# The lora outer products and the decay sum of an RWKV-7 layer, made per 512 tokens and passed through DRAM

## The chip, the cores and the metric

One core of one Trainium2 chip runs the whole program in one launch. The metric is device time in microseconds. The kernel before takes 3426.49 us (median of 3 runs, 3426.42 to 3430.7).

## The reference, cut to what matters

A two-layer decoder trunk over 1024 tokens of width 1024 in float32. Layer 0 mixes tokens with RWKV-7, layer 1 with gated DeltaNet; each is followed by a SwiGLU feed-forward of width 2816, with adaLN modulation and LayerNorm around them. The change touches layer 0 only:

```python
r = lerp(0) @ w_rkv[0]; k = lerp(1) @ w_rkv[1]; v = lerp(2) @ w_rkv[2]
w_log = -softplus(-(w0 + tanh(lerp(3) @ w1) @ w2)) - 0.5    # inner width 64
a = sigmoid(a0 + (lerp(4) @ a1) @ a2)                       # inner width 64
g = sigmoid(lerp(5) @ g1) @ g2                              # inner width 128
decay = exp(-exp(w_log))
# recurrence over tokens, per head of 64: S <- S*decay + (S a)b + v k
return (y * g) @ w_out
```

The three loras are `(… @ w1) @ w2`, `(… @ a1) @ a2` and `(… @ g1) @ g2`. Their first product is called the inner one, the second the outer one. The recurrence is run in chunks of 64 tokens; for that the kernel needs the running sum of `-log(decay)` inside each chunk, which it gets as a scan of `0.5*exp(-0.5)*(1 + tanh(z/2))`, with z the outer product plus `w0`.

## The kernel before, in words

Activations lie with channels on the 128 partitions (8 tiles `p` of 128 channels, each two heads) and tokens along the free dimension, in two halves `h` of 512 tokens. Every large product is done in three float32r matmuls (`mm3`, lines 261 to 263: high by high, high by low, low by high); weights are loaded by a DMA on SP's queue, cut into a high part by ACT (line 222 or 249) and a low part by POOL or DVE (line 212).

`proj_rwkv` makes, for each half, k, v and r in the order (h,1), (h,2), (h,0): for each `p` 24 matmuls of 512 columns into one PSUM bank `mm`, an ACT copy (line 471) and a store to DRAM (`rkv_d`, line 472). Beside v and r it accumulates the inner lora products in a bank `rows`, three matmuls of 512 columns for each `p`. At the end of a group the inner result `f` is cut into two parts kept in SBUF (`split_lora`).

The recurrence works on units: 256 tokens `q` of one `p` and half, 32 units in all, four of them in flight (`pairs`, with cut points `CUT`). `prep1` loads r, k, v from DRAM (line 994) and the norms (line 997), and builds the chunk matrices; `prep2` inverts; `chain` carries the state, normalizes, multiplies by the gate and stores `y` (line 1184). In the kernel before `prep1` also does, per unit, two `mm3` of 256 columns with the outer weights (loaded and cut at q == 0, line 1000), tanh on ACT, an affine step (line 196) and the scan (line 1024) on DVE; `chain` does a third `mm3` of 256 columns with the gate's weights (line 1171) into half of a PSUM bank `p1`.

The order of the instructions is written as Python generators that yield cost estimates; `weave` mixes two such generators by their estimated totals, and a list scheduler then orders each engine's queue ahead of time. On the chip every engine runs its queue in that fixed order. Four stretches matter here. First the projections of half 0 run alone, with the adaLN product (0 to about 235 us). Then the first 19 steps of the units are woven with the projections of half 1 (about 235 to 690). Then the other 16 steps are woven with layer 0's output projection and feed-forward of half 0 (to about 1380). Then the rest of layer 0 and layer 1.

Of the kernel before, what the change touches and what calls it, by code (L numbers as in the profile page):

```python
# [57 lines left out]
def body(ctx, tc, A):  # L58
# [23 lines left out]
    def tl(pl, shape, dt, tag, bufs=1):  # L82
        return pl.tile(shape, dt, tag=tag, name=nm(tag), bufs=bufs)
# [33 lines left out]
    def p1_ps():  # L117
        return bank("p1")
# [71 lines left out]
    def sigmoid(out, src, c=0.5, scale=0.5, hbias=None, d=None):  # L190

        if hbias is None:
            act.activation(out=out, in_=src, func=AF.Tanh, scale=scale)
        else:
            act.activation(out=out, in_=src, func=AF.Tanh, scale=scale, bias=hbias)
        dve.tensor_scalar(out=out, in0=out, scalar1=c, scalar2=c if d is None else d, op0=MUL, op1=ADD)
# [124 lines left out]
        return mod1[l][:, 24 * s + 16 + k:24 * s + 17 + k]  # L321

    rkv_d = [[[tl(dram, [P, HT], F32, f"rkv{h}{i}{p}") for p in range(KT)] for i in range(3)] for h in range(2)]
    y_d = [[[tl(dram, [P, HT], F32, f"y{l}{h}{p}") for p in range(KT)] for h in range(2)] for l in range(2)]
    kn_d = [tl(dram, [16, HT], F32, f"kn{h}") for h in range(2)]
    qk_d = [[tl(dram, [16, HT], F32, f"qk{h}{i}") for i in range(2)] for h in range(2)]
# [2 lines left out]
    A["taps"] = {"rkv": rkv_d, "y": y_d, "x2": x_d}  # L329

    utail = tl(cp, [P, KT], F32, "utail")

    lora = {}

    def sums(acc, sel, p, sq):

# [15 lines left out]
    def proj_rwkv():  # L352
# [88 lines left out]
        loaded.append(other_constants())  # L441
        for k in range(4, KT):
            lerp(0, 1, k)
        for (h, i), (h2, i2) in zip(order, order[1:]):
            a = [made[h, i, k] for k in range(KT)]
            acc = row_ps()
            for grp in GROUPS[h]:
                ws = {}
                for n in SMALL[i]:
                    lerp(h, 3 + n, grp[0])  # L450
                early = grp[0] in begun
                w = [None if early else weight(A["w_rkv"][i, p], (dve if p % SD[1] == 0 else pool) if h else None, ("r", i, p) if i != 1 or p >= NH else None) for p in grp]
                if h == 0:
                    ws = {n: small_weight(h, n, grp[0]) for n in SMALL[i]}
                pst = [begun.get(p) or mm_ps() for p in grp]
                if early:
                    half_product(grp[0], 1, ws0[grp[0]])
                    del begun[grp[0]]
                for k in range(KT):
                    for j in range(0 if early else len(grp)):  # L460
                        mm3(pst[j][:, :], w[j], P * k, a[k], k == 0, k == KT - 1)
                    if h and grp[-1] == KT - 1:
                        lerp(h2, i2, k)
                    if PY and k < KT - 1:
                        yield 0.65 * len(grp)
                for j, p in enumerate(grp):
                    if j:
                        for n in SMALL[i]:
                            lerp(h, 3 + n, p)
                    o = e_tile()  # L470
                    act.copy(out=o[:, :], in_=pst[j][:, :])
                    sync.dma_start(out=rkv_d[h][i][p][:, :], in_=o[:, :])
                    if i == 1:
                        sq = e_tile()
                        act.activation(out=sq[:, :], in_=pst[j][:, :], func=AF.Square, scale=V("kk", p))
                        sums(acc, C("hsel"), p, sq)
                    for n in SMALL[i]:
                        mm3(acc[:, :], ws.get(n) or small_weight(h, n, p), 0, made[h, 3 + n, p], p == 0 and n != 1, p == KT - 1 and n != 0)
                    if i == 0:
                        make_x(h + 1, p)  # L480
                    if h == 0:
                        lerp(h2, i2, p)
                    yield Part({1: 6.0, 2: 6.5, 0: 5.8}[i] - 7 * 0.65 * bool(PY))
            for k in range(KT):
                lerp(h2, i2, k)
            if i == 1:
                rows_out(kn_d[h], acc, 1e-6)
            else:
                f = inner[h, i] = tl(pools["pj"], [P, HT], F32, "f")
                if i == 2:  # L490
                    act.activation(out=f[0:64, :], in_=acc[0:64, :], func=AF.Tanh)
                    act.copy(out=f[64:P, :], in_=acc[64:P, :])
                else:
                    sigmoid(f[:, :], acc[:, :])
                if h == 0:
                    split_lora(h, i)

    loaded = []
    inner = {}

    def split_lora(h, i):

        t = lora.setdefault(h, {})
        f = inner.pop((h, i))
        t[i] = [tl(pools["l"], [P, HT], F32R, f"l{i}{e}")[:, :] for e in "hl"]
        split(f[:, :], *t[i])

    def lo_eng():
        flip[0] = (flip[0] + 1) % 3
# [215 lines left out]
          7: [1, 1, 1]}  # L725
    KNS = 17
    CS = [1.0, 1.0, 1.0]
    CUT = [14.0, 26.0, 41.0, 55.0]
    K = len(CUT)
    CUT[-1] = CUT[-1] + 0.0  # L730
    S2 = 3
# [2 lines left out]
    NC = [4, 3, 3, 3, 4]  # L734
    OP = ['u', '']
    NA = 0
    UC = 49.0
    GB = 1
    TI = 12
    TC = [1.0, 1.1, 1.0]  # L740
# [240 lines left out]
                live.remove(g)  # L981

    post_ps = {'p1': p1_ps, 'pa': pa_ps, 'pc': pc_ps, 'mm': mm_ps}['p1']
    gates = {}

    def prep1(rp, nb, ctxr, h, p, q, n, box):
        def r_tile(tag="t", n=nb["t"]):
            return tl(rp, [P, QT], F32, tag, n)

        tq = slice(QT * q, QT * q + QT)  # L990
        lrh, lrl = lora[h][2]
        r, k, v = r_tile("ld", nb["ld"]), r_tile("ld", nb["ld"]), r_tile("ld", nb["ld"])
        for i, t in ((1, k), (0, r), (2, v)):
            sync.dma_start(out=t[:, :], in_=rkv_d[h][i][p][:, tq])
        rb = r_tile("rb", 1)
        for j in range(2):
            sync.dma_start(out=rb[64 * j:64 * j + 64, :], in_=kn_d[h][2 * p + j:2 * p + j + 1, tq].to_broadcast([64, QT]))
        if q == 0:
            lw = tl(rp, [P, 2 * P], F32, "l2r", 1)
            sync.dma_start(out=lw[:, :], in_=A["w_l2"][p, :, 0:2 * P])  # L1000
            gates[p] = [(tl(rp, [P, 2 * P], F32R, "l2h", 2), tl(rp, [P, 2 * P], F32R, "l2l", 2))]
            split(lw[:, :], *(t[:, :] for t in gates[p][0]))
        wl2 = gates[p][0]
        lr = (lrh[:, tq], lrl[:, tq])
        pz = p1_ps()
        mm3(pz[:, 0:QT], wl2, 0, lr, True, True)
        dec = r_tile()
        if 'P' in OP[h]:
            act.activation(out=dec[:, :], in_=pz[:, 0:QT], func=AF.Tanh, scale=0.5, bias=vneg[:, p:p + 1])
            c = 0.5 * math.exp(-0.5)  # L1010
            pool.tensor_scalar(out=dec[:, :], in0=dec[:, :], scalar1=c, scalar2=c, op0=MUL, op1=ADD)
        elif 'd' in OP[h]:
            act.activation(out=dec[:, :], in_=pz[:, 0:QT], func=AF.Tanh, scale=0.5, bias=vneg[:, p:p + 1])
            act.activation(out=dec[:, :], in_=dec[:, :], func=AF.Identity, scale=0.5 * math.exp(-0.5), bias=bcol(5))
        else:
            sigmoid(dec[:, :], pz[:, 0:QT], c=0.5 * math.exp(-0.5), hbias=vneg[:, p:p + 1])
        yield 4.0
        pz = p1_ps()
        mm3(pz[:, 0:QT], wl2, P, lr, True, True)
        a = r_tile()  # L1020
        act.activation(out=a[:, :], in_=pz[:, 0:QT], func=AF.Tanh, scale=0.5, bias=vneg[:, 8 + p:9 + p])
        yield 1.0
        cum = r_tile()
        dve.tensor_tensor_scan(out=cum[:, :], data0=C("reset"), data1=dec[:, :], initial=0.0, op0=MUL, op1=ADD)
        e1 = tl(rp, [P, 4, 65], F32, "e1", nb["e1"])
        dve.memset(e1[:, :, 0:1], 1.0)
        act.activation(out=e1[:, :, 1:65], in_=v3(cum[:, :], 4), func=AF.Exp, scale=-1.0)
# [81 lines left out]
    def chain(rp, nb, ctxr, h, p, q, box):  # L1109
# [7 lines left out]
        for c in range(4):  # L1117
# [34 lines left out]
                stt(n0[hs, hs], pst[hs, hs], dcol[hs, c:c + 1], np_[hs, hs], MUL, ADD)  # L1152
            act.copy(out=yn[rr, P * i:P * i + P], in_=pq[rr, 0:P])
            yield 2.1
        y4 = v3(yn[:, :], 4)
        mean, var, tmp = (tl(rp, [P, 4], F32, n_, 2) for n_ in ("gm", "gv", "gt"))
        dve.tensor_reduce(out=mean[:, :], in_=y4, axis=mybir.AxisListType.X, op=ADD)
# [8 lines left out]
        newton(mean[:, :], var[:, :], tmp[:, :])  # L1166
        tt(dve, y4, y4, mean[:, :].unsqueeze(2).to_broadcast([P, 4, 64]), MUL)
        yield 2.1
        if q == 0:
            lw = tl(rp, [P, P], F32, "g2r", 1)  # L1170
            sync.dma_start(out=lw[:, :], in_=A["w_l2"][p, :, 2 * P:3 * P])
            gates[p].append((tl(rp, [P, P], F32R, "g2h", 2), tl(rp, [P, P], F32R, "g2l", 2)))
            split(lw[:, :], *(t[:, :] for t in gates[p][1]))
        wg = gates[p][1]
        lgh, lgl = lora[h][0]
        t = post_ps()
        for i in range(2):
            pe.transpose(t[:, P * i:P * i + P], yn[:, P * i:P * i + P], C("ident"))
        y = tl(rp, [P, QT], F32, "yo", nb["yo"])
        act.activation(out=y[:, :], in_=t[:, 0:QT], func=AF.Identity, bias=V("gnb", p), scale=V("gng", p))  # L1180
        tt(pool, y[:, :], y[:, :], bv[:, :], ADD)
        mm3(t[:, QT:2 * QT], wg, 0, (lgh[:, tq], lgl[:, tq]), True, True)
        tt(dve, y[:, :], y[:, :], t[:, QT:2 * QT], MUL)
        sync.dma_start(out=y_d[0][h][p][:, tq], in_=y[:, :])
        yield 4.2

    def pairs(rp, nb, ctxr):

# [260 lines left out]
    def main():  # L1449
        with tc.tile_pool(name="pj", bufs=1) as pools["pj"]:  # L1450
# [17 lines left out]
            steps = pairs(rp, nb, cr)  # L1468
            B = [2, 1, 1, 2, 2]
            banks(mm=B[0], rows=B[1], pa=B[2], p1=B[3], pc=B[4])  # L1470
            weave(seq(*steps[:SB]), 16 * UC * W[0], parts(proj, 3 * KT - PP), 112, LD[0])
            split_lora(1, 2)
            weave(seq(*steps[SB:SB + S2]), S2 * UC, proj, 34)
            split_lora(1, 0)
        pools["acc"] = ctx.enter_context(tc.tile_pool(name="acc", bufs=1, reuse_waits="tile"))
        B = [2, 1, 1, 2, 2]
        banks(mm=B[0], rows=B[1], pa=B[2], p1=B[3], pc=B[4])
# [138 lines left out]
```

## Time and profile before

| | |
|---|---|
| median of 3 runs | 3426.49 us |
| the profiled execution's own time | 3418.32 us |
| its span | 3416.5 us |
| TensorE busy | 3229.8 us, 19408 matmuls |
| DVE / ACT / POOL busy | 2207.9 / 1374.5 / 974.0 us |
| mean granted TensorE clock | 0.97 |
| moved by DMA | 594.12 MB |

PE is the matmul engine, PEld its weight loads, SPq the queue from which the DMAs are issued. A matmul's shown duration includes its pipeline, so neighbours overlap: what one takes from PE is read from the start of one matmul to the start of the next. "[5.58 <-ACT l2h L222]" behind a row says that the engine stood idle for 5.58 us before it and what it waited for.

### The profile page before, as it was taken

Reading aid. Unit: us, or ns where it says so; the run is one execution under the profiler, and the core shown is the slowest. Engines: PE = TensorE matmul, PEld = TensorE weight load, DVE = VectorE, ACT = ScalarE, POOL = GpSimd, SP = SyncE. Lnnn points to the kernel's source line nnn. Section 1 sums busy time; section 2 is a strip of 40 time slices with the busy share of each in tenths; the row PEclk is TensorE's granted clock in tenths of the full one; section 3 lists DMA queues with packets and bytes.
Section 4 is the critical chain, followed back from the end, with each engine's and each line's share of the span. In section 5 each row is a group of like instructions: output and inputs, shape, how many; then the busy total and the mean of one; then the engine's idle time right before and its main releaser. Section 6 shows DMA issues by size and latency. Waiting matters only on the chain. (4 is left out here: it accounts for less than half of the span.)

```text
span 3416.5 us, 51830 instructions
## 1 busy us (share of the span) xinstructions
PE 3229.8 (95%) x19408; PEld 2464.8 (72%) x19408; DVE 2207.9 (65%) x4630; ACT 1374.5 (40%) x2622; POOL 974.0 (29%) x725
## 2 busy tenths in 40 slices
PE   7989999988999999988999999999989999999997
PEld 3667777765666676766777777777767778878886
DVE  5667888877666666587676555586577763573235
ACT  4656777634333333344332222345323223342222
POOL 2443233343333333443321000220133333420001
PEclk8999999997999999999999999999999999999998
DMA  7872334352444444644664554556644446565543
GB/s 260 274 242 89 114 106 132 122 171 82 159 148 165 145 165 141 217 165 175 223 209 166 182 170 168 199 187 218 223 166 157 151 151 235 182 209 185 197 174 135
DMA packets 240524, 594.12 MB, mean 174 GB/s; under 512 B 24720, under 2 KB 80656, under 8 KB 240272
## 3 DMA queue, kind: packets, MB, share of 16 engines
q1 hardware_dynamic: 240128, 590.74, 51.1%
q8 instruction: 152, 2.49, 0.3%
q14 instruction: 100, 0.82, 0.1%
q10 hardware_dynamic: 144, 0.07, 0.0%
HBM read 440.04 MB, written 150.67 MB: 173 GB/s over the span
## 5 line engine op out<-in xcount | busy, mean ns | idle before, releaser
L261 PE MATMUL mm<-s,wh 128*128 128x512 f32 x2608 | 1081.3, 415 | 14.0 <-DVE s L224 5.9
L262 PE MATMUL mm<-s,wh 128*128 128x512 f32 x2608 | 1057.9, 406 | 14.6 <-DVE s L212 8.2
L263 PE MATMUL mm<-s,wl 128*128 128x512 f32 x2608 | 1050.0, 403 | 0.0
L212 POOL TENSOR_TENSOR wl<-wr,wh 128x1024 fp32r<-128x1024 f32 (+1 forms) x243 | 504.4, 2082 | 981.9 <-ACT wh L222 912.4
L261 PEld LDWEIGHTS mm<-s,wh 128*128 128x128 f32 x2608 | 497.4, 191 | 129.2 <-issue 19.8
L262 PEld LDWEIGHTS mm<-s,wh 128*128 128x128 f32 x2608 | 498.4, 191 | 112.3 <-DVE s L212 12.7
L263 PEld LDWEIGHTS mm<-s,wl 128*128 128x128 f32 x2608 | 497.5, 191 | 95.1 <-issue 1.2
L249 ACT CAST wh<-wr 128x1024 fp32r<-128x1024 f32 x199 | 206.6, 1049 | 500.4 <-PE mm L262 260.3
L222 ACT CAST wh<-wr 128x1024 fp32r<-128x1024 f32 (+1 forms) x254 | 228.2, 905 | 343.9 <-PE mm L262 201.1
L215 DVE SCALAR_TENSOR_TENSOR x<-mm,modp,x 128x512 f32<-128x512 f32 x272 | 202.1, 747 | 73.9 <-PE mm L263 72.0
L261 PE MATMUL mm<-ys,wh 128*128 128x512 f32 x544 | 219.6, 404 | 2.9 <-DVE x L215 2.8
L262 PE MATMUL mm<-ys,wh 128*128 128x512 f32 x544 | 217.3, 400 | 0.0
L263 PE MATMUL mm<-ys,wl 128*128 128x512 f32 x544 | 217.3, 399 | 0.0
L212 DVE TENSOR_TENSOR e<-mm,e 128x512 f32<-128x512 f32 x88 | 60.6, 689 | 168.7 <-PE mm L263 168.4
L212 DVE TENSOR_TENSOR s<-e,s 128x512 fp32r<-128x512 f32 x106 | 122.2, 1154 | 60.8 <-ACT s L222 60.6
L833 PEld LDWEIGHTS <-z 128*128 128x128 f16 x1600 | 83.8, 98 | 103.3 <-issue 64.2
L215 DVE SCALAR_TENSOR_TENSOR e<-e,mm 128x512 f32<-128x512 f32 x88 | 60.2, 684 | 141.8 <-ACT e L676 141.4
L215 DVE SCALAR_TENSOR_TENSOR tx<-mm,modp,tx 128x512 f32<-128x512 f32 x112 | 83.1, 748 | 79.4 <-PE mm L263 79.1
L261 PEld LDWEIGHTS mm<-ys,wh 128*128 128x128 f32 x544 | 103.7, 191 | 29.7 <-DVE x L215 3.7
L263 PEld LDWEIGHTS mm<-ys,wl 128*128 128x128 f32 x544 | 103.5, 190 | 25.7
L262 PEld LDWEIGHTS mm<-ys,wh 128*128 128x128 f32 x544 | 103.7, 191 | 25.2 <-issue 0.5
L215 DVE SCALAR_TENSOR_TENSOR e<-e,vec,e 128x512 f32<-128x512 f32 x144 | 115.0, 799 | 3.8
(389 smaller groups left out, 5418.8 us busy)
## 6 DMA issues: line engine op xcount, KB each, us to landing
wr<-w_in SPq DMA_DIRECT2D x176, 512.0 KB, 4.5
ada<-ada_w SPq DMA_DIRECT2D x96, 512.0 KB, 4.8
loi<-wl SPq DMA_DIRECT2D x88, 512.0 KB, 3.0
wr<-w_ffo SPq DMA_DIRECT2D x88, 512.0 KB, 4.9
wl<-loi SPq DMA_DIRECT2D x88, 512.0 KB, 3.6
wr<-w_g SPq DMA_DIRECT2D x64, 512.0 KB, 4.5
lof<-wl SPq DMA_DIRECT2D x44, 512.0 KB, 2.9
wl<-lof SPq DMA_DIRECT2D x44, 512.0 KB, 3.5
```

The lines of the kernel that those rows point to most:

```text
L212: eng.tensor_tensor(out=out, in0=a, in1=b, op=op)
L215: return dve.scalar_tensor_tensor(out=out, in0=a, scalar=s, in1=b, op0=op0, op1=op1)
L222: act.copy(out=hi, in_=src)
L249: act.copy(out=hi[:, :], in_=raw[:, :])
L261: pe.matmul(out, wh[:, off:off + P], ah, start=start, stop=False)
L262: pe.matmul(out, wh[:, off:off + P], al, start=False, stop=False)
L263: pe.matmul(out, wl[:, off:off + P], ah, start=False, stop=stop)
L833: pe.matmul(out, l, r, start=start, stop=stop)
```

## The change

A new DRAM array `lo_d` holds, for each half and `p`, the running sum, the tanh of `a` and the gate. `outer(h, i, p)` makes them for 512 tokens at a time, inside `proj_rwkv`; `prep1` and `chain` load 256 tokens of them for a unit. The inner parts are now in one pair of tiles, used by one lora after the other.

```diff
+        def outer(h, i, p):
+            n = 2 if i == 2 else 1
+            raw = tl(pools["pj"], [P, 2 * P], F32, "l2r")
+            sync.dma_start(out=raw[:, 0:P * n], in_=A["w_l2"][p, :, (0 if n == 2 else 2 * P):P * (2 if n == 2 else 3)])
+            w = [tl(pools["pj"], [P, 2 * P], F32R, "l2" + e) for e in "hl"]
+            split(raw[:, 0:P * n], *(t[:, 0:P * n] for t in w))
+            for j in range(n):
+                ps = mm_ps()
+                mm3(ps[:, :], w, P * j, inner[h, i], True, True)
+                o = e_tile()
+                if n == 1:
+                    act.copy(out=o, in_=ps[:, :])
+                elif j == 0:
+                    dec = e_tile()
+                    sigmoid(dec, ps[:, :], c=0.5 * math.exp(-0.5), hbias=vneg[:, p:p + 1])
+                    for q in range(2):
+                        tq = slice(256 * q, 256 * q + 256)
+                        dve.tensor_tensor_scan(out=o[:, tq], data0=C("reset"), data1=dec[:, tq], initial=0.0, op0=MUL, op1=ADD)
+                else:
+                    act.activation(out=o, in_=ps[:, :], func=AF.Tanh, scale=0.5, bias=vneg[:, 8 + p:9 + p])
+                sync.dma_start(out=lo_d[h][j if n == 2 else 2][p][:, :], in_=o)
+            yield 0.7 * n
...
                     yield Part({1: 6.0, 2: 6.5, 0: 5.8}[i] - 7 * 0.65 * bool(PY))
+                    if i == 0 and (h == 0 or p < 4):
+                        for pair in (p,) if h == 0 else (2 * p, 2 * p + 1):
+                            yield from outer(h, 2, pair)
+                    if h == 1 and i == 1 and p < 4:
+                        for pair in (2 * p, 2 * p + 1):
+                            yield from outer(0, 0, pair)
...
+            if h == 1 and i == 0:
+                for p in range(KT):
+                    yield from outer(1, 0, p)
...
-    CUT = [14.0, 26.0, 41.0, 55.0]
+    CUT = [12.0, 24.0, 39.0, 52.5]
-    UC = 49.0
+    UC = 46.5
...
-        lrh, lrl = lora[h][2]
...
-        pz = p1_ps()
-        mm3(pz[:, 0:QT], wl2, 0, lr, True, True)
-        dec = r_tile()
...
-            sigmoid(dec[:, :], pz[:, 0:QT], c=0.5 * math.exp(-0.5), hbias=vneg[:, p:p + 1])
-        yield 4.0
-        pz = p1_ps()
-        mm3(pz[:, 0:QT], wl2, P, lr, True, True)
-        a = r_tile()
-        act.activation(out=a[:, :], in_=pz[:, 0:QT], func=AF.Tanh, scale=0.5, bias=vneg[:, 8 + p:9 + p])
-        yield 1.0
-        cum = r_tile()
-        dve.tensor_tensor_scan(out=cum[:, :], data0=C("reset"), data1=dec[:, :], initial=0.0, op0=MUL, op1=ADD)
+        cum, a = tl(rp, [P, QT], F32, "cl", 2), tl(rp, [P, QT], F32, "al", 2)
+        for i, t in enumerate((cum, a)):
+            sync.dma_start(out=t[:, :], in_=lo_d[h][i][p][:, tq])
+        yield 3.0
...
+        gl = tl(rp, [P, QT], F32, "gl", 2)
+        sync.dma_start(out=gl[:, :], in_=lo_d[h][2][p][:, tq])
...
-        mm3(t[:, QT:2 * QT], wg, 0, (lgh[:, tq], lgl[:, tq]), True, True)
-        tt(dve, y[:, :], y[:, :], t[:, QT:2 * QT], MUL)
+        tt(dve, y[:, :], y[:, :], gl[:, :], MUL)
         sync.dma_start(out=y_d[0][h][p][:, tq], in_=y[:, :])
-        yield 4.2
+        yield 3.5
...
-            weave(seq(*steps[:SB]), 16 * UC * W[0], parts(proj, 3 * KT - PP), 112, LD[0])
-            split_lora(1, 2)
-            weave(seq(*steps[SB:SB + S2]), S2 * UC, proj, 34)
-            split_lora(1, 0)
+            weave(seq(*steps[:SB]), 16 * UC * W[0], parts(proj, 3 * KT - PP), 120, LD[0])
+            weave(seq(*steps[SB:SB + S2]), S2 * UC, proj, 48)
```

## Rows read from the trace of the kernel before

**Rows 1.** The page, part 1: busy time of the matmul engine and the others.
```profile
PE 3229.8 (95%) x19408; PEld 2464.8 (72%) x19408; DVE 2207.9 (65%) x4630; ACT 1374.5 (40%) x2622; POOL 974.0 (29%) x725
```

**Rows 2.** Windows: stretch, length, busy us of each engine, granted clock, DMA share, GB/s.
```profile
0.00:235.00 235.00, 206.40 (x970) 139.20 (x971) 140.53 (x219) 130.91 (x225) 86.85 (x72) 0.94 0.78 268
175.00:235.00 60.00, 56.92 (x267) 43.50 (x266) 40.39 (x54) 35.45 (x60) 25.92 (x20) 1.00 0.79 267
235.00:690.00 455.00, 437.03 (x4165) 329.41 (x4163) 372.45 (x1031) 310.82 (x816) 149.15 (x187) 0.98 0.37 116
400.00:560.00 160.00, 156.98 (x1507) 119.15 (x1504) 139.97 (x397) 119.19 (x310) 48.37 (x65) 1.00 0.35 112
690.00:1380.00 690.00, 643.48 (x4297) 463.06 (x4298) 477.14 (x1187) 237.49 (x498) 263.64 (x205) 0.94 0.44 145
```

**Rows 3.** Waits of PE from 235 to 690 us: total, times, longest.
```profile
PE p L261 <- ACT l2h L222: 5.6, 1, 5.6
PE p L1057 <- DVE t L1055: 2.8, 2, 1.6
```

**Rows 4.** The weights' tiles: outer matmuls; count, ns min/median/max, first and last start.
```profile
L261 PE MATMUL p<-l2h,l2h x64: 274/364/582, 241.9 to 1266.5; 128*128 128x256 f32 x64
L261 PE MATMUL p<-l0h,g2h x32: 278/282/418, 308.7 to 1374.1; 128*128 128x256 f32 x32
L261 PE MATMUL rows<-sm,wh x24: 389/389/395, 110.2 to 230.3; 128*128 128x512 f32 x24
L261 PE MATMUL rows<-s,wh x24: 390/474/503, 393.0 to 669.0; 128*128 128x512 f32 x24
```

**Rows 5.** Timeline of PE at 409 us (start, duration, instruction): one gate product.
```profile
409.30 0.28 PE L261 MATMUL p<-l0h,g2h 128*128 128x256 f32 x1
409.42 0.28 PE L262 MATMUL p<-l0l,g2h 128*128 128x256 f32 x1
409.54 0.28 PE L263 MATMUL p<-l0h,g2l 128*128 128x256 f32 x1
```

**Rows 6.** Timeline of PE at 218 us: one inner product and the matmul behind it.
```profile
217.63 0.39 PE L261 MATMUL rows<-sm,wh 128*128 128x512 f32 x1
217.86 0.40 PE L262 MATMUL rows<-sm,wh 128*128 128x512 f32 x1
218.10 0.39 PE L263 MATMUL rows<-sm,wl 128*128 128x512 f32 x1
218.33 0.40 PE L261 MATMUL mm<-sx,wh 128*128 128x512 f32 x1
```

**Rows 7.** Timelines of PE and POOL where the units begin.
```profile
235.93 0.39 PE L262 MATMUL mm<-s,wh 128*128 128x512 f32 x1
241.90 0.58 PE L261 MATMUL p<-l2h,l2h 128*128 128x256 f32 x1 [5.58 <-ACT l2h L222]
...
248.20 0.43 PE L338 MATMUL rows<-e,cst 128*32 128x128 f32 x8
...
250.94 0.70 PE L1057 MATMUL p<-t,cst 128*128 128x256 f32 x2 [1.64 <-DVE t L1055]
...
244.28 2.76 POOL L212 TENSOR_TENSOR wl<-wr,wh 128x1024 fp32r<-128x1024 f32 x1 [1.21 <-ACT t L1021]
```

**Rows 8.** Groups by line: shapes, count, busy us, mean ns, idle before.
```profile
L1024 DVE TENSOR_TENSOR_SCAN t<-cst,t 128x256 f32<-128x256 f32 x32 | 27.5, 859 | 0.6
L212 POOL TENSOR_TENSOR l2l<-l2r,l2h 128x256 fp32r<-128x256 f32 x16 | 14.1, 880 | 29.1 <-ACT l2h L222 26.5 <-PE p L263 2.6
L471 ACT COPY e<-mm 128x512 f32<-128x512 f32 x48 | 27.8, 580 | 12.1 <-PE mm L263 11.6
```

**Rows 9.** DMA issues: count, KB each, median us from issue to landing.
```profile
rkv<-e SPq DMA_DIRECT2D x48, 256.0 KB, 3.4
ld<-rkv SPq DMA_DIRECT2D x96, 128.0 KB, 2.3
l2r<-w_l SPq DMA_DIRECT2D x16, 128.0 KB, 2.1
```

More of the change, by code (lines that the diff above doesn't have):

```diff
@@ L323, in body @@
     rkv_d = [[[tl(dram, [P, HT], F32, f"rkv{h}{i}{p}") for p in range(KT)] for i in range(3)] for h in range(2)]
+    lo_d = [[[tl(dram, [P, HT], F32, f"lora{h}{i}{p}") for p in range(KT)] for i in range(3)] for h in range(2)]
     y_d = [[[tl(dram, [P, HT], F32, f"y{l}{h}{p}") for p in range(KT)] for h in range(2)] for l in range(2)]
@@ L331, in body @@
     utail = tl(cp, [P, KT], F32, "utail")
-    lora = {}
     def sums(acc, sel, p, sq):
@@ L443, in proj_rwkv, with inner_parts @@
             lerp(0, 1, k)
+        def inner_parts(h, i, acc):
+            f = tl(pools["pj"], [P, HT], F32, "f")
+            if i == 2:
+                act.activation(out=f[0:64, :], in_=acc[0:64, :], func=AF.Tanh)
+                act.copy(out=f[64:P, :], in_=acc[64:P, :])
+            else:
+                sigmoid(f[:, :], acc[:, :])
+            t = tuple(tl(pools["l"], [P, HT], F32R, f"l{e}")[:, :] for e in "hl")
+            split(f[:, :], *t)
+            inner[h, i] = t
+        def outer(h, i, p):
[16 more added lines that the diff above has]
+                        dve.tensor_tensor_scan(out=o[:, tq], data0=C("reset"), data1=dec[:, tq], initial=0.0, op0=MUL, op1=ADD)
+                else:
+                    act.activation(out=o, in_=ps[:, :], func=AF.Tanh, scale=0.5, bias=vneg[:, 8 + p:9 + p])
+                sync.dma_start(out=lo_d[h][j if n == 2 else 2][p][:, :], in_=o)
+            yield 0.7 * n
         for (h, i), (h2, i2) in zip(order, order[1:]):
@@ L488, in proj_rwkv @@
             else:
[L489 to L496, printed above, removed]
+                inner_parts(h, i, acc)
+            if h == 1 and i == 0:
+                for p in range(KT):
+                    yield from outer(1, 0, p)
     loaded = []
     inner = {}
[L501 to L506, printed above, removed]
     def lo_eng():
@@ L983, in body @@
     post_ps = {'p1': p1_ps, 'pa': pa_ps, 'pc': pc_ps, 'mm': mm_ps}['p1']
-    gates = {}
     def prep1(rp, nb, ctxr, h, p, q, n, box):
@@ L997, in prep1 @@
             sync.dma_start(out=rb[64 * j:64 * j + 64, :], in_=kn_d[h][2 * p + j:2 * p + j + 1, tq].to_broadcast([64, QT]))
[L998 to L1004, printed above, removed]
-        pz = p1_ps()
-        mm3(pz[:, 0:QT], wl2, 0, lr, True, True)
-        dec = r_tile()
[L1008 to L1015, printed above, removed]
-            sigmoid(dec[:, :], pz[:, 0:QT], c=0.5 * math.exp(-0.5), hbias=vneg[:, p:p + 1])
-        yield 4.0
-        pz = p1_ps()
-        mm3(pz[:, 0:QT], wl2, P, lr, True, True)
-        a = r_tile()
-        act.activation(out=a[:, :], in_=pz[:, 0:QT], func=AF.Tanh, scale=0.5, bias=vneg[:, 8 + p:9 + p])
-        yield 1.0
-        cum = r_tile()
-        dve.tensor_tensor_scan(out=cum[:, :], data0=C("reset"), data1=dec[:, :], initial=0.0, op0=MUL, op1=ADD)
+        cum, a = tl(rp, [P, QT], F32, "cl", 2), tl(rp, [P, QT], F32, "al", 2)
+        for i, t in enumerate((cum, a)):
+            sync.dma_start(out=t[:, :], in_=lo_d[h][i][p][:, tq])
+        yield 3.0
         e1 = tl(rp, [P, 4, 65], F32, "e1", nb["e1"])
@@ L1168, in chain @@
         yield 2.1
[L1169 to L1175, printed above, removed]
         t = post_ps()
```

## The prediction

> **What bounds the kernel now.** I read the busy table first: the matmul engine PE is busy for 3229.8 us of a span of 3416.5, the next engine, DVE, for 65% [rows 1]. Then the windows, cut where the program changes stage [rows 2]. In all three stages that the change touches PE is the fullest engine: 437 of 455 us where the units are woven with half 1's projections, 157 of 160 us in the middle of that, 643 of 690 us in the stage behind it. DVE is second; it comes near PE only in the middle stage (140 of 160). Third the waits of PE: from 235 to 690 us the longest is a single one of 5.6 us, at the start of the units, and behind it come 2.8 us in two waits [rows 3]. So PE's fixed order is nearly always filled, and an edit is worth here what it takes from PE's queue, in start-to-start time, and little else.
>
> **The change, part by part.**
>
> *PE, what goes.* 64 products of three 256-column matmuls for decay and `a`, and 32 for the gate [rows 4]. Alone, three of these take 0.36 us (starts at 409.30, 409.42, 409.54, 120 ns apart) [rows 5]. Most stand alone between matmuls of other shapes, so I added up, in PE's timeline, the time from each start to the next matmul's start for all of them, from the first at 241.9 us to the last at 1374.1 [rows 4]: 39 of the 64 lie before 690 us and take 19.8 us, 25 behind it 13.9 us; 16 gates before 690 us take 7.2 us and 16 behind it 8.5 us. Together 49.3 us, 0.51 for each product: 0.36 of work and 0.15 of entering and leaving.
>
> *PE, what comes.* 48 products of three 512-column matmuls. The trace has the same thing, the inner lora products. Those of half 0, between matmuls of their own kind, take 0.70 us (217.63 to 218.33) [rows 6], on the mean of 24 0.683 us. The 24 of half 1, among the units' matmuls [rows 4], take 0.846 us in the same sum of starts. The change puts 16 (decay and `a`, half 0) into the first stage and 32 into the second: 16 × 0.683 = 10.9 and 32 × 0.846 = 27.1, 38.0 us together. By stage: +10.9 up to 235 us, +27.1 − 19.8 − 7.2 = +0.1 to 690 us, −22.4 behind it. Net −11.4 us. Bounds: if all new products lie between their own kind, 48 × 0.683 = 32.8 and −16.5. If what the old ones pay for entering is paid by their neighbours anyway, 96 × 0.36 − 32.8 gives −1.8.
>
> A rule of the Trainium skill speaks for that upper end: "TensorE: Matmul & The Clock Gate", section Back-to-back issue gap, gives an isolated matmul N/2.4 + 2.5 ns at the full clock. By it 288 matmuls of 256 columns cost 31.4 us and 144 of 512 columns 31.1 us, an estimate that leaves 0.3 us for the merging. The rows say 120 ns and 227 to 230 ns, some 10 ns more a matmul [rows 5, 6], and the rule has no term for a change of shape.
>
> *The later stage's share.* The −22.4 us are gained only if PE's waits there don't grow by as much. That stage has 46.5 us of idle PE in 690 [rows 2]. With less matmul work between the units' dependent steps I let waits grow by a fifth of what goes: +4.5 us. Bounds 0 and +22.4 (the stage wholly bound by the units' own chain).
>
> *Where the units begin.* PE stands for 5.58 us before the first outer product, since its weights come late on SP's queue, and 1.64 us before line 1057 [rows 7]. Both products and their weights go from there. But PE doesn't get all of it back: half 1's second weight waits for POOL, which cuts it at 244.28 to 247.04, behind the outer weights [rows 7]. Without these (two cuts of 128×256 at 0.88 us [rows 8], one for the gate and their waits, some 3 us) that weight is ready at about 244, and PE has half a product (2.6 us) and the last outer products (1.4 us) until then. So the first product ends at about 249.4 us with both done, against 248.2 with one done, where its sums of squares follow [rows 7]: a gain of 24 × 0.227 − 1.2 = 4.2 us. I take −4; bounds 0 (the stall moves to line 1057, which now waits for two more loads) and −7.2, the sum of both waits.
>
> *What the outer products wait for.* Each needs a load (2.1 us to landing [rows 9]), an ACT cut (0.4, an estimate from 0.58 for a copy of 512 columns) and a POOL cut (0.88 [rows 8]), 3.4 us, in single buffers. The inner weights go the same way now, and no wait of PE on their products is among the waits [rows 3]; a product's period is 8 × 0.683 + 0.683 = 6.1 us, longer than the chain. What hides it is PE's own product; without that cover it costs 3.4 us a time, 24 × 3.4 = 82 us at most and nothing at least. I take +2 for both stages, near the inner weights' row.
>
> *PSUM banks.* The new products use the two banks `mm` that the projections alternate between; the next product must wait until ACT has copied (0.58 us [rows 8]). In the middle stage the units' matmuls stand between; in the first there are five banks. 0, with at most 32 × 0.58 = 19 us.
>
> *DVE, ACT, POOL.* 32 scans of 256 stay 32 scans of 256 (0.86 us [rows 8]); 32 affine steps become 16 of 512, the gate's multiply reads SBUF for PSUM. ACT loses 64 short tanh and gets 32 long ones and 16 copies, about the same time. POOL's cuts stay 32. In the first stage DVE gets 8 × 2 × 0.86 = 14 us of scans and some 4 us of affine steps (an estimate), 18 us, on top of 40 in 60 [rows 2], in a stretch that becomes 71 us: 82%. Off the path, 0; at most those 18 us.
>
> *DMA and SP.* 48 stores of 256 KB and 96 loads of 128 KB are new, 144 issues, 25 MB. For 175 to 235 us, the fullest stretch, 4.2 MB of stores and 1 MB of weights on top of 267 GB/s × 60 us = 16 MB make 21.3 MB in 71 us, 299 GB/s, where a share of 0.79 now goes with 267 [rows 2], so 338 would be full. A load lands 2.3 us after its issue, a store 3.4 us [rows 9], and half 0's values are written tens of microseconds before their first unit. Only unit 16 reads what was just written: load, cuts, product, tanh, two scans, store and load are some 13 us, in a step of about 30 us with three other units in flight. 0; at most 13 us once.
>
> *Sum:* −11.4 + 4.5 − 4 + 2 = −8.9 us, all on PE. The profiled execution took 3418.32 us for its span of 3416.5, 8.2 us under the median of the timed runs, 3426.49. The difference is carried to the median: 3426.5 − 8.9 = 3417.6, in round figures 3417 us.
>
> **The rivals.**
>
> *A. No gain.* PE streams the same number of columns, and the entering is paid by the neighbours: −1.8 in place of −11.4. Then the waits have nothing to refill. With −4 + 2 that is −3.8, or 3422.7 us. For it: rows 5 and 6, 240 ns for two halves against 227. Against it: 0.51 against 0.36 over 96 products. The Trainium skill's rule above says the same.
>
> *B. Slower.* In the stretch from 175 to 235 us nothing but the projection's own matmuls stands between PE and a late outer product, and the outer weights have one buffer each. SP's queue is in order: the two stores of one outer product wait there for the tanh and the scans, and behind them wait the next 512 KB weight and the next outer weight. The point from which it decides: scans that end later than a product's period, 6.1 us, less the 3.4 us of the chain. Price: 3.4 us for each of 8 products there and of the 8 that the last group appends with no projection beside them, 16 × 3.4 = 54 at most; half of that, 27, on top of −8.9 gives +18, or 3444.6 us. For it: DMA share 0.79 there, DVE on its way to 82%. Against it: the inner weights' products take 0.683 us in just this stretch, with no wait.
>
> *C. A larger gain.* The waits behind 690 us shrink with the work: fewer steps hand over between PE, ACT and DVE (three products a unit less, two PSUM banks less used), and PE at 0.94 of its clock there [rows 2] spends 12% of the stage at 1.2 GHz. −16.5 − 7.2 on PE and a tenth of the 46.5 us idle and of the roughly 41 us that the low clock costs, −9: −33, or 3394 us at the end; the middle of the case is 3402.
>
> **How the numbers follow.** Forecast 0.38, A 0.20, B 0.22, C 0.20. A measurement of this kernel tells about 0.2% from no change, 6.9 us: faster is under 3419.6, slower over 3433.3. The forecast's own range is 3409 to 3425, with two thirds of it faster (0.25 faster, 0.13 same). A is the same (0.18; 0.02 faster), C faster (0.20), B slower (0.20; 0.02 same). Faster 0.47, same 0.33, slower 0.20; I move 0.04 from same to slower, since the order of all queues up to 1380 us is made anew and the terms are small. Range 3394 to 3444: from the far end of C to the price of B, a tenth left out at either side.
>
> **What would show it.** The start-to-start sum of the 48 new products near 38 us, none with a wait over 1 us before it; the units beginning some 10 us later than 235, with no wait of 5 us on PE; the last store of half 0's k, v, r some 11 to 14 us later; the stretch from the start of the units' second part to the last `y` of half 1 some 18 us shorter. Wrong it is if PE waits for `l2h` or `l2l` between 175 and 250 us again and again, if SP's waits for the new stores stand at the head of its list and weight loads behind them, or if the later stage keeps its length.

## The result: slower by 1%

The changed kernel takes 3458.23 us (median of 4 runs, 3456.07 to 3459.83), the kernel before 3426.45 in the same runs (3422.1 to 3430.7): ratio 1.0099, 95% interval 1.0081 to 1.0117, some 34 us slower. The forecast was 3417 and its range ended at 3444. The profiled execution has a span of 3458.1 us against 3416.5.

The busy table after, part 1 of the page [rows 1]:

```profile
PE 3261.4 (94%) x19264; PEld 2471.4 (71%) x19264; DVE 2216.0 (64%) x4614; ACT 1375.2 (40%) x2606; POOL 973.9 (28%) x725
```

PE streams the same columns in 144 fewer matmuls, yet is busy 31.6 us longer. DVE, ACT and POOL are where they were. The windows after, in the stretches of [rows 2] (length, busy of PE, PEld, DVE, ACT, POOL, granted clock, DMA share, GB/s):

```profile
0.00:235.00 235.00, 204.11 (x942) 135.07 (x943) 138.92 (x224) 130.50 (x229) 84.63 (x71) 0.93 0.78 270
175.00:235.00 60.00, 53.91 (x237) 39.22 (x236) 37.52 (x59) 35.34 (x64) 22.71 (x18) 0.97 0.82 281
235.00:690.00 455.00, 431.53 (x3857) 317.47 (x3856) 360.38 (x965) 299.89 (x774) 137.48 (x180) 0.95 0.44 140
400.00:560.00 160.00, 157.26 (x1476) 115.09 (x1476) 139.05 (x381) 116.82 (x297) 42.30 (x58) 1.00 0.39 120
690.00:1380.00 690.00, 644.29 (x4298) 457.91 (x4296) 476.90 (x1166) 239.60 (x500) 265.43 (x206) 0.93 0.47 158
```

From 235 to 690 us PE does 308 matmuls fewer than before in almost the same busy time, at 0.95 of its clock for 0.98. The middle (400 to 560) is as full as it was, so the trouble lies behind it. PE's waits there, the two largest [rows 3]:

```profile
PE pa L863 <- DVE jx L936: 4.8, 7, 2.5
PE pc L1128 <- DVE ar L212: 3.7, 1, 3.7
```

The wait for the outer weights (5.6 us before) is gone, as forecast, and two thirds of it are back as a wait for `ar` at the units' start. No wait is large. What is lost is seen in milestones, the times at which SP issues a unit's first load, the `y` stores of some units (numbered from 0) and half 0's first load for the output projection:

| us | first load | unit 0 | 9 | 13 | 15 | 17 | 31 | output projection |
|---|---|---|---|---|---|---|---|---|
| before | 234.0 | 310 | 529 | 633 | 678 | 768 | 1377 | 667 |
| after | 249.9 | 317 | 542 | 646 | 717 | 827 | 1418 | 762 |
| later: "spread" | 247.7 | 318 | 542 | 642 | 697 | 806 | 1396 | 742 |

The first load comes 16 us late; unit 0's `y` is only 7 us late, so 9 are won back at once. Then 7 are lost up to unit 13 and 46 from unit 13 to unit 17, and 19 are won back behind it. Two stores of half 1's r, 564.23 and 620.22 us, lie 56 us apart; before, no two in a row lie more than 22.4 apart. In that hole (the same columns; before, after):

```profile
570.00:600.00 30.00, 29.36 (x270) 21.67 (x269) 26.74 (x70) 21.99 (x58) 12.49 (x17) 1.00 0.47 149
```
```profile
570.00:600.00 30.00, 24.94 (x228) 19.97 (x229) 22.19 (x68) 15.65 (x44) 8.36 (x12) 0.72 0.26 80
580.00:590.00 10.00, 7.11 (x90) 5.44 (x90) 7.71 (x31) 3.84 (x13) 0.73 (x1) 0.82 0.12 41
590.00:600.00 10.00, 8.84 (x49) 7.03 (x51) 6.19 (x16) 4.04 (x11) 2.07 (x3) 0.50 0.23 65
```

Every engine and the DMAs are less busy, and the granted clock falls to 0.50, the lower level of 1.2 GHz, after PE has stood for 2.9 us of the ten before. PE's timeline shows what is missing: from 569 to 607 us one matmul of 512 columns, where before there were 65. The last outer products ahead of the hole and the first behind it, on PE, then their readers on ACT and on DVE (start, duration, instruction):

```profile
565.13 0.47 PE L261 MATMUL mm<-lh,l2h 128*128 128x512 f32 x1
...
565.90 0.47 PE L263 MATMUL mm<-lh,l2l 128*128 128x512 f32 x1
...
567.98 0.51 PE L261 MATMUL mm<-lh,l2h 128*128 128x512 f32 x1
...
568.79 0.49 PE L263 MATMUL mm<-lh,l2l 128*128 128x512 f32 x1
...
607.30 0.50 PE L261 MATMUL mm<-lh,l2h 128*128 128x512 f32 x1
...
608.11 0.39 PE L261 MATMUL mm<-s,wh 128*128 128x512 f32 x1
```
```profile
565.26 0.69 ACT L195 ACTIVATE e<-mm,vneg 128x512 f32<-128x512 f32 x1
...
605.30 0.69 ACT L476 ACTIVATE e<-mm,vneg 128x512 f32<-128x512 f32 x1
605.88 0.69 ACT L195 ACTIVATE e<-mm,vneg 128x512 f32<-128x512 f32 x1
```
```profile
591.53 0.43 DVE L196 TENSOR_SCALAR e<-e 128x512 f32<-128x512 f32 x1
...
605.20 0.68 DVE L474 TENSOR_TENSOR_SCAN e<-cst,e 128x256 f32<-128x256 f32 x1
```

The product for `a` of pair 0 is done at 566.4 us and the one for the decay of pair 1 at 569.3; each holds one of the two `mm` banks until ACT reads it, at 605.30 and 605.88. Until then the r product, PE's only other filler, can't start. ACT is not busy in between (15.65 of 30 us): these reads stand late in its fixed order, and the affine step and scan of pair 0 late in DVE's.

The new products [rows 4, 6], first the tile's row with its weights, then the first product:

```profile
L261 PE MATMUL mm<-lh,l2h x48: 391/477/793, 178.8 to 758.8; 128*128 128x512 f32 x48
```
```profile
178.82 0.40 PE L261 MATMUL mm<-lh,l2h 128*128 128x512 f32 x1
179.05 0.39 PE L262 MATMUL mm<-ll,l2h 128*128 128x512 f32 x1
179.29 0.39 PE L263 MATMUL mm<-lh,l2l 128*128 128x512 f32 x1
179.52 0.39 PE L261 MATMUL mm<-lh,l2h 128*128 128x512 f32 x1
```

And the new transfers [rows 9] (count, KB each, median us to landing):

```profile
lora<-e SPq DMA_DIRECT2D x48, 256.0 KB, 2.6
cl<-lora SPq DMA_DIRECT2D x32, 128.0 KB, 2.6
```

### The profile page after: what moved, and what is told of

Same layout as the page of the kernel before. It is cut to its first block, busy times and chain, and to the rows that moved or that the text cites. A ratio compares the mean times of both kernels' runs of the same rounds, so it can differ in the third digit from the quotient of the medians.

```text
span 3458.1 us, 51694 instructions
## 1 busy us (share of the span) xinstructions
PE 3261.4 (94%) x19264; PEld 2471.4 (71%) x19264; DVE 2216.0 (64%) x4614; ACT 1375.2 (40%) x2606; POOL 973.9 (28%) x725
```

## The experiments

Three theories stood at the start, for the 46 us. **T1:** the outer products' results wait, for a place in SBUF or for their turn on ACT and DVE, and hold the two `mm` banks. **T2:** the added traffic or its place in SP's queue makes the projection's weights late. **T3:** the estimates with which the projections are woven into the units make them run out early. All ratios are to runs of the kernel before on the same chip; medians of different runs come in part from different chips, so runs are compared with each other by their ratios.

**1. Own tiles for the results.**

```diff
-                o = e_tile()
+                o = e_tile() if "lo" not in pools else tl(pools["lo"], [P, HT], F32, "lo", 2)[:, :]
...
-                    dec = e_tile()
+                    dec = e_tile() if "lo" not in pools else tl(pools["lo"], [P, HT], F32, "dec", 1)[:, :]
```

> In the second stretch the outer products' results and the decay tile get tiles of their own (two and one) instead of the five shared e tiles; nothing else changes. Theory T1 (in 565 to 605 us both mm banks are held by outer products whose results have no tile to go to, so that the projection of r behind them can't run; that is most of the 46 us lost between the 13th and the 17th store of y): the banks come free at once, 20 to 40 us come back, 3420 to 3438 us. T2 (the stores and loads through SP's queue hold the weights back): no change, 3458. T3 (the weave's totals let the filling work run out): no change, 3458.

3475.26 us, ratio 1.0152 (1.0132 to 1.0172): slower than the change itself. The three outer products now stand at 569.4, 572.0 and 574.8 us and the next matmul into `mm` comes 38 us after the last of them. The tanh for `a` of pair 0 now has a tile free for it and still comes at 612.95 us, so a place in SBUF is not what it waits for. For the decay of pair 1 this run doesn't exclude it: the single `dec` tile is in use until 615.9 us, and ACT reads the bank at 616.06.

**2. Other banks.** All outer products but those of the first stretch go to the units' `p1` banks.

```diff
-                ps = mm_ps()
+                ps = (mm_ps if (h, i) == (0, 2) else p1_ps)()
```

> All outer products but those of half 0's decay and a write to the two p1 banks of the units instead of the two mm banks. T1: the projection of r runs on through 565 to 605 us, but the units may now wait for p1; 15 to 40 us come back, 3418 to 3443 us. T2 and T3: no change, 3458 us.

3467.29 us, 1.0129 (1.0112 to 1.0147). The windows of this kernel:

```profile
570.00:600.00 30.00, 29.50 (x273) 21.73 (x272) 24.97 (x76) 20.15 (x51) 7.83 (x11) 1.00 0.57 182
600.00:630.00 30.00, 27.42 (x246) 21.09 (x246) 23.41 (x65) 18.77 (x53) 10.88 (x14) 0.77 0.23 72
```

The r product runs on at full clock to 593 us; then the hole comes all the same, 30 us later, and the stores of r lie at 565 and 634. Now both `mm` banks are held by the r product itself: ACT's next copy of it comes at 633.11 us, behind its reads of the outer products (623.85 to 629.14). So a held bank is how the delay reaches PE, and another bank for the outer products only puts it off.

**3. The new stores on ACT's queue** (`act.dma_start` for `sync.dma_start` in `outer`).

> The 48 stores of the outer products' results are issued from ACT's queue instead of SP's. T2: weights are no longer behind these stores; 20 us or more come back, 3438 us or less. T1 and T3: within 10 us of 3458, since the banks are held as before; ACT pays the issue of 48 transfers.

3464.94 us (3455.43 to 3474.64), 1.0123 (1.0097 to 1.015), with the hole in its place (stores of r at 567 and 623 us) and the last store of half 0's k, v, r at 249.54 us (249.46 with the change). SP's order is not the cause of either. The Trainium skill's "DMA: Bandwidth & Descriptors", Rules for kernel authors, says that spreading DMAs over several issuing engines gains no bandwidth. In time this run agrees, though from 175 to 235 us it moved 296 GB/s for 281.

**4. The traffic alone**, in the kernel before: each k, v, r tile is stored twice, and each unit loads three tiles more that nothing uses.

```diff
                     sync.dma_start(out=rkv_d[h][i][p][:, :], in_=o[:, :])
+                    sync.dma_start(out=lo_d[h][i][p][:, :], in_=o[:, :])
...
+        for i, t in ((0, "cl"), (1, "al"), (2, "gl")):
+            sync.dma_start(out=tl(rp, [P, QT], F32, t, 1)[:, :], in_=lo_d[h][i][p][:, tq])
```

> The kernel before, with as many transfers as the change adds: each of the 48 results of k, v, r is stored a second time (256 KB) to an array of its own, and each unit loads 256 tokens of three of these (128 KB each, 96 in all) into tiles that nothing reads. T2: 20 us or more slower than before, 3446 or more. T1 and T3: within 8 us of before, 3420 to 3434 us.

3449.86 us, 1.0078 (1.0063 to 1.0093). The time is what T2 expected, but its place is not: the first load moves from 234.0 to 266.3 us (+32), unit 0's `y` is 31 us late, unit 15's 25, the last one 31, with no hole in the stores of r (at most 25 us apart). From unit 13 to unit 17 it loses 10 us against the kernel before, where the change loses 46. So T2 falls for the hole; in the first stretch the 6.3 MB of stores cost 32 us.

**5. The weave's estimate**: the first weave is planned with 104 for the projections, not 120.

> One number is changed: the first weave of units and half 1's projections is planned with 104 for the projections in place of 120, so the projections are handed out more slowly and should last to the end of the sixteenth step. T3 (the projections run out of order before the units' steps do, so PE has nothing to fill in between 565 and 605 us and its clock falls): the gap in the stores of half 1's r, 56 us now, is under 30, unit 17's y leaves before 800 us (827 now), and the time is 15 to 35 us below the changed kernel's 3458, near 3425 to 3440. T1 (the outer products hold the two banks that the projection needs, until ACT and DVE come to them behind the units' work): the gap only moves with the place of the outer products, and the time stays within 10 us of 3458.

3456.06 us, 1.0087 (1.0065 to 1.0108), level with the change. The gap in the stores of r falls from 56 to 29 us (601, 631), as T3 had it, though two pairs still follow each of r's first four parts. But unit 17's `y` leaves at 821 us, not below 800, and the granted clock from 570 to 600 us is still 0.77: the same filler is spread more thinly. T3 has a hand in the hole, not in the time.

**6. Gates in the units**, decay, sum and `a` by the new way (cut to its core; the inner parts of the gates get tiles of their own again, and the planned totals of both weaves are set for it, to 114 and 42).

```diff
-        sync.dma_start(out=gl[:, :], in_=lo_d[h][2][p][:, tq])
...
-        tt(dve, y[:, :], y[:, :], gl[:, :], MUL)
+        mm3(t[:, QT:2 * QT], wg, 0, (lgh[:, tq], lgl[:, tq]), True, True)
+        tt(dve, y[:, :], y[:, :], t[:, QT:2 * QT], MUL)
```

> Decay, running sum and a go by the new way; the gates stay in the units as in the kernel before (16 outer products of 512 columns and 16 stores less, 32 products of 256 columns more). If the gates' outer products behind the projection (730 to 762 us, nothing beside them) and in the product of k are the loss: near the kernel before, 3425 to 3435. If it is the decay's and a's products of half 1 beside the product of r (T1, T3): within 10 us of 3458, unit 17's y still behind 815 us.

3452.43 us, 1.008 (1.0057 to 1.0103): by its time the second case, with unit 17's `y` at 812 us, a little before the 815 that it named. The gates are not the main loss.

**7. The burst spread**: half 1's decay and `a` come one pair behind each of r's eight parts, not two behind each of the first four.

```diff
-                    if i == 0 and (h == 0 or p < 4):
-                        for pair in (p,) if h == 0 else (2 * p, 2 * p + 1):
-                            yield from outer(h, 2, pair)
+                    if i == 0:
+                        yield from outer(h, 2, p)
```

> Half 1's outer products for decay and a come one pair behind each of the eight parts of the product of r, not two pairs behind each of the first four. T1 (six outer products in a row take both banks while DVE and ACT are behind): with two in a row instead of four the gap in the stores of half 1's r is halved, to 25 to 35 us, and the time is 10 to 25 us below 3458. T3 (the planned ratio): the first two outer products are where they were, the gap stays over 45 us and the time within 8 us of 3458.

3442.84 us (3434.12 to 3452.32), 1.0051 (1.0033 to 1.0069): 15 us back, as T1 had it. The stores of r lie 25 us apart (564.13, 589.41), and the hole is filled, with 46 matmuls of 512 columns from 569 to 607 us, six of them outer products:

```profile
570.00:600.00 30.00, 29.00 (x282) 21.27 (x282) 27.24 (x77) 20.53 (x56) 11.20 (x15) 1.00 0.52 169
```

**8. Spread and 104 together.**

> Both edits: 104 for the first weave and one pair of outer products behind each part of r. If both causes act, it is the fastest of the four, 3420 to 3435, that is level with the kernel before; if T3 alone acts, it is within 6 us of the kernel with 104 alone; if T1 alone, within 6 us of the spread one.

3445.31 us, 1.0054 (1.0034 to 1.0073), level with 7: T1 alone.

**9. Less in the first stretch**: 7, and of half 0's decay and `a` only two pairs in the first stretch, the other six behind half 1's k. For this the inner parts get a pair of tiles for each lora, and the first weave is planned with 128, not 120.

```diff
+                    if i == 0 and (h == 1 or p < 2):
+                        yield from outer(h, 2, p)
+                    if h == 1 and i == 1:
+                        if p < 6:
+                            yield from outer(0, 2, p + 2)
+                        yield from outer(0, 0, p)
```

> The spread kernel (one pair of outer products behind each part of half 1's r, 3443) with one more move: of half 0's decay and a only the first two pairs are made in the first stretch, the other six behind the parts of half 1's k, each with one gate. If what the first stretch lost (its end 14 us later than before) is the outer products' own work and traffic there: the units begin at 236 to 240 us and not 248, and the time is 3430 to 3440, some 3 to 12 us below the spread kernel, since the same PE work comes back in the middle stage at a higher price (0.85 for 0.68 us). If the end of the first stretch is late for another reason (half 1's first weight, SP's order), the units begin at 245 or later and the time is 3443 or more.

3452.74 us, 1.0097 (1.0081 to 1.0112): by the ratios 16 us slower than 7. The units begin at 240.65, near the 236 to 240 expected, but unit 0's `y` leaves at 317, where it was: PE stands for 8.3 us, up to 249.05, for a tile that ACT squares late (line 510), and what was won is used up at once. That the moved work costs more between the units is a reading; the 128 is not tested by itself.

**10. Half 1's gates back in the units**, on top of 7 (the second weave planned with 42, not 48); **11.** 9 and 10 together.

```diff
+        if h == 0:
             gl = tl(rp, [P, QT], F32, "gl", 2)
...
-            if h == 1 and i == 0:
-                for p in range(KT):
-                    yield from outer(1, 0, p)
```

> The spread kernel with the gates of half 1 alone back in the units (8 outer products and 8 stores less, 16 products of 256 columns more); half 0's gates still go through DRAM. If the eight gates behind the last projection (724 to 742 us, nothing but the units beside them, and units 16 and 17 waiting for the first of them) cost time by themselves: from unit 16's to unit 17's y some 50 us in place of 75, and 3425 to 3437. If that interval only shows when the projections end: within 5 us of 3443.

> Both moves together. If both of the causes above act, 3418 to 3430, level with the kernel before (3426) or a little below it; if only one does, the time of the better of the two.

3438.63 us, 1.0054 (1.0037 to 1.0071), and 3449.38, 1.0084 (1.0071 to 1.0097). From unit 16's to unit 17's `y` it is 48 us in 10, as before the change (720.37 to 767.86), against 77 after. But unit 16's `y` comes 22 us later than in 7 (753 for 731), and the time is that of 7 within its interval: the order there changes, the sum does not.

**12 to 14. What PE's work is worth where.** 12 and 13 change the kernel before (one, and six, matmuls in place of three in each of the units' 96 products), 14 changes 7 (one in place of three in each of the 48 new ones).

```diff
+    def mm1(out, w, off, a, start, stop):
+        pe.matmul(out, w[0][:, off:off + P], a[0], start=start, stop=stop)
...
-        mm3(pz[:, 0:QT], wl2, 0, lr, True, True)
+        mm1(pz[:, 0:QT], wl2, 0, lr, True, True)
```

> The kernel before; each of the units' 96 lora products is one matmul of 256 columns and not three (the two that correct for rounding are left out), so 192 matmuls at 0.12 us, 23 us of PE, go, and the places where PE enters and leaves a product stay. If PE's queue sets the time (the forecast's term): 18 to 25 us below the kernel before, 3400 to 3408. If what goes from PE between the units' dependent steps comes back as waits or as a lower clock: less than 10 us below.

> The kernel before; each of the 96 products is made twice over in the same bank, 288 matmuls of 256 columns at 0.12 us more, 35 us of PE. If PE's queue sets the time: 30 to 38 us above the kernel before, 3455 to 3463. If the extra matmuls fill places where PE would wait: under 20 us above.

> The spread kernel; each of the 48 new outer products is one matmul of 512 columns and not three, 96 matmuls at 0.23 us, 22 us of PE, fewer: 7 in the first stretch, 15 beside half 1's projections. If these products cost what their matmuls take: 15 to 22 us below the spread kernel, 3421 to 3428. If their cost is the place that they take in the order (stalls before and behind them, late weights and results): under 8 us below.

12: 3412.68 us, ratio 0.9975 (0.9957 to 0.9992), so 8.6 us (3 to 15) for 23 us of matmuls taken away, the second case. 13: 3450.62, 1.0092 (1.0072 to 1.0111), so 31 us (25 to 38) for 35 us added, the first case. 14: 3424.46, 1.0015 (1.0 to 1.0029), against 1.0051 for 7: 12 us (some 4 to 20) for 22 taken away, between its two cases. In this kernel work added to the units costs most of its length; of work taken from them about a third comes back.

## Why the prediction was wrong, step by step

PE's account up to the first `yr<-y` load, which comes just behind the last `y` store, summed over windows of 5 us: idle time; busy time times the share of the clock that was not granted; and the rest, the work at full clock.

| us | until | idle | low clock | full-clock work |
|---|---|---|---|---|
| before | 1380 | 93 | 47 | 1240 |
| after | 1419 | 102 | 70 | 1247 |
| 7, spread | 1397 | 102 | 47 | 1248 |
| 12, before with one matmul | 1370 | 99 | 52 | 1218 |
| 13, before with six | 1413 | 96 | 44 | 1273 |

Of the 39 us some 23 are low clock, 8 work and 9 idle, and the profile of 7 has none of the 23. But each row is one execution, and the granted clock differs between executions of one kernel: that of 7 took 3434.12 us at 0.973 (medians of its six runs: 3442.84 and 0.9685), and that of 8, at 3454.24 us and 0.962 (medians 3445.31 and 0.968), has 72 us of low clock without the hole. So what the hole costs is better read in its own place, from 565 to 620 us (after; 7):

```profile
565.00:620.00 55.00, 49.94 (x446) 38.28 (x444) 42.93 (x132) 32.26 (x89) 13.71 (x19) 0.78 0.33 104
565.00:620.00 55.00, 52.96 (x502) 38.71 (x502) 48.20 (x141) 39.44 (x104) 16.51 (x24) 1.00 0.53 168
```

That is 11 us of low clock (0.22 of 49.94) and 3 us more of idle time, 14 together, near the 15 us that spreading won back in the timed runs. The Trainium skill's "TensorE: Matmul & The Clock Gate", section HAM oscillation, says that a kernel in which PE keeps stopping for its next operands runs its matmuls at the low clock, and that the loop should be rearranged so that PE is fed. The page's case is a wait for loads; here PE lacked its filler. The rows of 570 to 600 us, 0.72 with the burst and 1.00 without, agree with the remedy.

**The failed step: "PSUM banks ... 0"**, with "in the middle stage the units' matmuls stand between" as its reason. They stand between, but ACT's and DVE's orders stand between as well: a bank was held not for the 0.58 us of a copy, which gave the bound of 19 us, but for 37 to 39 us, because the readers of four products in a row had their turn late. The step looked at how long an instruction takes, not at where it stands in its engine's order. Spreading them won 15 us (7); tiles of their own (1), another bank (2), another queue (3) and the estimate (5) did not, and the traffic alone (4) made no hole. This step explains 15 of the 34 us; the next one failed as well.

**PE's sum, −11.4 us, was not there.** The start-to-start sum of the new products, forecast at 38.0, is 54.3: 15.2 up to 250 us (16 products; 10.9 forecast, the difference two waits behind them of some 2 us each), 27.7 to 690 us (24 products, one followed by 3.8 us of waiting), 11.4 behind (8 gates, nothing but the units beside them). And the units' own matmuls, unchanged in number, became dearer, in the same start-to-start sums:

| from `y` of unit to unit | before | after | 7, spread |
|---|---|---|---|
| 0 to 9 | 111.6 us, 67 ns each | 119.5, 70 | 119.2, 69 |
| 9 to 13 | 52.0, 69 | 67.6, 91 | 53.3, 71 |
| 15 to 17 | 22.7, 81 | 40.9, 127 | 39.2, 123 |
| all, to 1424 us | 410.8 | 448.4 | 429.7 |

The first line fits rival A, taken too lightly: of the 0.15 us of entering that each removed product was credited with, its neighbours seem to go on paying a part, some 3 ns for each of the units' matmuls. No run tests this by itself. The second is the hole. The third is the end of the projections: before, dense work comes in from 667 us, while the last of r is still being made; after it comes at 762, 40 us behind the last of r, and in between the units run with little beside them, at 127 ns a matmul. Run 12 gives the price: PE's full-clock work falls by 22 us there, idle and low clock rise by 11, and the time falls by a third of what was taken. "An edit is worth here what it takes from PE's queue" holds nearly for work added (13), not for work removed between the units' dependent steps.

**Where the units begin.** Forecast "some 10 us later", found 15.9 by the first load; the last store of half 0's k, v, r is 12.6 later (236.89 to 249.46), inside its 11 to 14. Up to unit 0's `y` 9 us are regained from the first load, 6 from the last store, for a forecast of 4 with a far bound of 7.2. The net, +7 at unit 0, was forecast, but from the wrong resource, so that agreement is luck. Run 14 takes some 7 us of PE's work from the first stretch and its end stays where it was; run 4 adds only stores and the end moves by 32 us:

```profile
247.70 1.52 SPq L1020 DMA_DIRECT2D ld<-rkv  x3
```
```profile
247.71 1.40 SPq L1023 DMA_DIRECT2D ld<-rkv  x3
```
```profile
266.33 1.60 SPq L996 DMA_DIRECT2D ld<-rkv  x3
```

(7, 14 and 4.) So the end there goes with what is stored, not with PE's matmuls; whether by the rate of the DMAs or by the order of the issues is not shown. "338 would be full" was an extrapolation; with 21 MB asked for, the stretch from 175 to 235 us went from 267 to 281 GB/s at a share of 0.82.

**The weights' chain, +2.** Right in kind: no wait for `l2h` or `l2l` above 1 us up to 250 us; behind 690 the gates, in single buffers with no projection beside them, are 3 to 6 us apart. Its far bound was counted short: there are 32 such loads, not 24.

**The later stage, −18.** Right: from unit 17 to unit 31 it is 590 us for 609. But 46 us had been lost before it.

**Rivals.** B forecast the right side by another mechanism. Its sign did come: from 175 to 250 us the wait for the new stores stands at the head of SP's list.

```profile
SPq L477 <- DVE e L474: 15.0, 6, 3.3
```

But with these stores on ACT's queue (3) the last store and the time stayed, and DVE, forecast at 82% there, was busy for 51.05 of these 75 us, 68%. So SP's queue was not the cause. C did not come.

**What stays open.** The spread kernel is still 17 us above the kernel before. By the rates of 12 and 14, the matmul time taken away (96 × 0.36 = 35 us, at 8.6 of 23) is worth 13 us and that added (48 × 0.70 = 34 us, at 12 of 22) costs 18, together +5, an estimate with wide intervals. The other 12 lie in the waits, the traffic of the first stretch and the end of the projections, which these runs don't separate. Nor is it shown why the list scheduler gave ACT's and DVE's reads so late a place. No version here that does all the work beats the kernel before.

## What to carry to other kernels

Where a product's result goes through few banks in a kernel with a fixed order, ask when its reader has its turn, not how long it takes, and try not to put more of them in a row than there are banks. Price work removed from between dependent steps at less than its length unless something else is ready to run there: here a third came back, while work added cost most of its length. A filler that now ends later than the next one begins leaves the steps between them uncovered.

## What was not expected of the hardware

A stretch in which PE was still busy for 24.94 of 30 us had a granted clock of 0.72, with 0.50 in its last ten us; from 565 to 620 us losing the filler cost more through the clock (11 us) than through idle time (3 us). And with 48 doubled stores and 96 loads (run 4) 32 us were lost ahead of the units, at a DMA share of 0.80 from 175 to 235 us, and none in sum from unit 0 to unit 31, at a share of 0.51 from 235 to 690 us.
